# Layer 1's output gate, summed over partitions by block transposes and a selection matrix and spread through DRAM, in a two-layer diffusion trunk

## The chip, the core and the metric

The kernel runs on one core of one Trainium2 chip. The metric is device time in microseconds (us) for one execution. Before the change the median of three runs is 1133.07 us (1133.02 to 1134.05).

Engine names are those of the profile: PE is the matrix engine (PEld its weight loads), DVE the vector engine, ACT the scalar engine, POOL the general-purpose engine, SP the engine that issues nearly all DMA transfers. Each engine runs its own instructions in a fixed order. DMA transfers are issued by SP in that same manner: a transfer that has to wait for something holds back everything behind it on SP.

## The reference, cut to what matters

Two layers of the block below run on a latent stream of 256 tokens and a context of 256 tokens, width 2048, all in float32. The change concerns only the line that makes `gate` for the second layer (l = 1) and its use in the last line.

```python
for l in range(DEPTH):                      # DEPTH = 2
    shift, scale, gate = jnp.split(silu_c @ w_mod[l] + b_mod[l], 3, axis=-1)
    ...
    h = rmsnorm(x, g_pre[l]) * (1.0 + scale[:, None]) + shift[:, None]
    proj = h @ w_in[l]
    ...
    y = mixer_branches(proj, latent_attn, g_sgu[l], w_sgu[l], b_sgu[l], w_fourier[l], b_fourier[l])
    y = rmsnorm(y @ w_out[l], g_post[l])
    x_new = x + gate[:, None] * y
```

So `gate` of layer 1 is a vector of 2048 values: a product of a vector of 2048 with a 2048 x 2048 matrix, plus a bias. The kernel multiplies it by `g_post[1]` at once, and uses the product on every token row of the last projection's result.

## The kernel before

**The last stage.** `finish()` (from line 1134) is the last projection, `y @ w_out[1]`. The 2048 output columns are done in four chunks c of 512. In a chunk, the contraction runs over 16 tiles k of 128, and for each k two token tiles t of 128 rows are done; one product is three matmuls (high times high, high times low, low times high), since every float32 operand is split into two parts of a faster type. In chunk 3 the second token tile runs 8 steps of k behind the first (`BACK = 8`), so that the first one's result can be written out while the second is still being multiplied.

**The weight stream.** `W` loads weights in units of 512 KB; a unit of this stage holds two tiles k of one chunk, so a chunk takes eight units. A unit passes through three steps: SP issues the load into one of three `raw` buffers (line 433), ACT casts the high part out of it (`whi`, line 456), DVE subtracts to get the low part (`wlo`, line 458), after which the `raw` buffer is free. Four `whi` and four `wlo` buffers hold the split units until PE has used them. The last six units go to other places (`TAIL`, line 383), because chunk 3 keeps its units for a second pass: the pair hl0 to hl3, the pair hl4 to hl7, mraw, then macc with `ws bsb`, and two in yo buffers. So the tags `ws` and `bsb` are used in two ways: by the gate, and as the low part of the fourth of these units.

**The gate.** `mod_gate1` (line 280) makes the product with the matrix on DVE, in between other work: for each chunk c it accumulates 16 multiply-adds (lines 289 and 291) of 128 x 512 into a tile (`ctrh`, `ctrl`, `nstrh`, `nstrl` for c = 0 to 3). What is left is a sum over the 128 partitions. `gate1(c)` (line 298) does that, with the bias and `g_post`:

- SP loads two rows, bias and `g_post`, each spread to all 128 partitions, 256 KB each (line 302), into `ws` and `bsb`.
- ACT and DVE split the accumulated tile into two parts (lines 505 and 506).
- PE multiplies a matrix of ones by both parts (line 307), two matmuls of 512 columns. Every partition of the result then has the sum.
- DVE adds the bias row (line 308) and multiplies by the `g_post` row (line 309).

**Who uses it.** `evac(c, t)` (line 1166) multiplies the projection's result by `g1[c]` on DVE (line 1170) for c = 0 to 2, as soon as the 16 steps of one token tile are done; `close(t)` (line 1176) does it for c = 3 (line 1183) and writes the outputs.

**The order.** PE's order is written out by hand. Work that runs beside the matmuls is a generator handed to `later`; each step k moves the planner's clock on, and a generator goes on at the next step after its delay. `GATES` (line 336) says after which step each gate is begun: gate 0 after k = 2 of chunk 0, gate 1 after k = 14 of chunk 0, gate 2 after k = 14 of chunk 1, gate 3 after k = 12 of chunk 2. Between the two parts of `gate1` lie 6.5 planner units (`YG`), some six steps k. On the other engines and on SP the order is made by a list scheduler at build time, from its own estimate of when each instruction can run. So on SP a transfer may stand ahead of its place in the program text, but once the order is made, it is kept.

A second routine, `mod_end` (line 270), already sums other modulation vectors over partitions in another way: two DVE instructions of `mod_dve` (lines 259 and 260) transpose the accumulated tile in blocks of 32 x 32 and sum 32 elements each, and four small matmuls with the 128 x 32 selection matrix `selq` (line 273) add up the four blocks of partitions and put the result into columns, one value a partition. `Mod.cols` (line 189) uses the same four matmuls (line 193) with four columns.

Of the kernel before, what the change touches and what calls it, by code (L numbers as in the profile page):

```python
# [7 lines left out]
F32 = mybir.dt.float32  # L8
F32R = mybir.dt.float32r
BF16 = mybir.dt.bfloat16  # L10
AF = mybir.ActivationFunctionType
ALU = mybir.AluOpType

P = 128
# [52 lines left out]
def trunk_kernel(ctx: ExitStack, tc: tile.TileContext, xT, xhalf, cT, wss, wsl, wmod, win, wout0, wout1, const, vec, rows,  # L67
                 wmat, bs, sink, out):
    nc = tc.nc
    V, A, G, PE, DMA = nc.vector, nc.scalar, nc.gpsimd, nc.tensor, nc.sync  # L70

    pool = ctx.enter_context(tc.tile_pool(name="sb", bufs=1))
    psum = ctx.enter_context(tc.tile_pool(name="ps", bufs=1, space=bass.MemoryType.PSUM))
    W2K = 7
    cnt = [0]

    def sb(shape, dt, tag, bufs=1):
        cnt[0] += 1
        return pool.tile(shape, dt, tag=tag, bufs=bufs, name=f"{tag}_{cnt[0]}")

    def w2k(shape, dt=F32):
        return sb(shape, dt, "w2k", W2K)

# [4 lines left out]
    def ms_ps(name="ms"):  # L88
        cnt[0] += 1
        return psum.tile([P, 512], F32, tag="ms", bufs=2, name=f"ps_{name}_{cnt[0]}")  # L90
# [6 lines left out]
    ones = sb([P, P], F32, "ones")  # L97
# [29 lines left out]
    def cc(name):  # L127
        o, w = COFF[name]
        return cst[:, o - P:o - P + w]

    def vc(l, name):
        o, w = VOFF[name]
        return vecs[:, l, o:o + w]
# [8 lines left out]
    g1 = []  # L142
# [154 lines left out]

    def gate1(c):

        r = [sb([P, 512], F32, tag) for tag in ("ws", "bsb")]  # L300
        for i in range(2):
            DMA.dma_start(r[i], rows[None, i, c * 512:(c + 1) * 512].to_broadcast([P, 512]))
        parts = split_into(w2k([P, 512], F32R), w2k([P, 512], F32R), g1[c])
        yield YG
        ps = ms_ps("gate")
        for i, t in enumerate(parts):
            PE.matmul(ps, state["ones"], t, start=i == 0, stop=i == 1)
        V.tensor_tensor(out=g1[c], in0=r[0], in1=ps, op=ALU.add)
        V.tensor_tensor(out=g1[c], in0=g1[c], in1=r[1], op=ALU.mult)
        yield 0.0  # L310

    def mod_rest():
# [7 lines left out]
    state = {"ctx": [], "phase": "", "owed": 0.0}  # L320
# [183 lines left out]
    def split_into(hi, lo, src):  # L504
        A.copy(hi, src)  # L505
        V.tensor_tensor(out=lo, in0=src, in1=hi.bitcast(F32), op=ALU.subtract)  # L506
        return hi, lo
# [626 lines left out]
    def finish():  # L1134
# [68 lines left out]
        for c in range(4):  # L1203
            pss = [mm_ps("y") for _ in range(2)]
            back = BACK if c == 3 else 0
            w = []
            for k in range(KT + back):
                if k < KT:
                    if k % 2 == 0:
                        w.append(W.next())  # L1210
                    products(c, k, 0, pss[0])
                if k == KT - 1:
                    evac(c, 0, pss[0])
                    if c == 3:
                        close(0, pss[0])
                if k >= back:
                    products(c, k - back, 1, pss[1])
                later.tick(PASS * 1024)
                if k in GATES[c]:
                    later.add(gate1(GATES[c][k]))  # L1220
            evac(c, 1, pss[1])
# [93 lines left out]
    with tc.manual_schedule(engines={EN.PE}):  # L1315
# [12 lines left out]
        for k in range(KT):  # L1328
            q = w2k([P, T])
# [3 lines left out]
            c = slice(32 * (k % 4), 32 * (k % 4) + 32)  # L1333
# [3 lines left out]
        row = w2k([P, T])  # L1337
# [6 lines left out]
        ps = ms_ps("rs")  # L1344
# [99 lines left out]
```

## Time and profile before

| | us |
|---|---|
| median of three runs | 1133.07 |
| lowest and highest run | 1133.02, 1134.05 |
| the profiled execution's own time | 1132.31 |
| its span, first to last instruction | 1130.5 |
| PE busy | 1122.0 |
| DVE busy | 927.6 |
| ACT busy | 528.5 |
| chunks 0, 1, 2 of the last stage begin on PE at about | 1029.5, 1053.7, 1077.9 |
| chunk 3 begins, and PE's last product ends, at about | 1100.0, 1122.7 |

Times inside the trace count from the first instruction of the profiled execution. A row of a timeline has the start, the length, the engine, the line of the kernel, the operation, and output and input tiles; a bracket at its end tells how long the engine was idle before it and what ended that. In a matmul's row the length is that of one instruction from its start to its end in a pipeline; the distance from one start to the next is what it costs PE. The granted clock of PE reads 1.00 in all four chunks.

### The profile page before, as it was taken

Reading aid. Unit: us, or ns where it says so; the run is one execution under the profiler, and the core shown is the slowest. Engines: PE = TensorE matmul, PEld = TensorE weight load, DVE = VectorE, ACT = ScalarE, POOL = GpSimd, SP = SyncE. Lnnn points to the kernel's source line nnn. Section 1 sums busy time; section 2 is a strip of 40 time slices with the busy share of each in tenths; the row PEclk is TensorE's granted clock in tenths of the full one; section 3 lists DMA queues with packets and bytes.
Section 4 is the critical chain, followed back from the end, with each engine's and each line's share of the span. In section 5 each row is a group of like instructions: output and inputs, shape, how many; then the busy total and the mean of one; then the engine's idle time right before and its main releaser. Section 6 shows DMA issues by size and latency. Waiting matters only on the chain.

```text
span 1130.5 us, 16656 instructions
## 1 busy us (share of the span) xinstructions
PE 1122.0 (99%) x6117; PEld 921.5 (82%) x6117; DVE 927.6 (82%) x1649; ACT 528.5 (47%) x991; POOL 33.7 (3%) x41
## 2 busy tenths in 40 slices
PE   8999999999999999999999999999999999999998
PEld 3666788888888888888888888988888888888886
DVE  1578799989888788898999988397889789878883
ACT  5322433322235666642533334256665369857551
POOL 0000000000000000000000000030500000000000
PEclk9999999999999999999999999999999999999999
DMA  9999656566656344356556665276956686556972
GB/s 350 403 402 400 243 181 202 170 206 192 215 175 188 107 140 131 122 180 211 186 170 223 221 212 179 94 170 213 226 168 197 214 295 195 158 170 198 315 251 75
DMA packets 75250, 235.85 MB, mean 209 GB/s; under 512 B 8736, under 2 KB 13216, under 8 KB 75168
## 3 DMA queue, kind: packets, MB, share of 16 engines
q1 hardware_dynamic: 70992, 230.85, 61.4%
q0 software_dynamic: 4032, 3.67, 2.2%
q8 instruction: 48, 0.79, 0.3%
q14 instruction: 34, 0.28, 0.1%
q10 hardware_dynamic: 144, 0.26, 0.1%
HBM read 232.65 MB, written 2.10 MB: 208 GB/s over the span
## 4 chain that ended last, share of the span: by engine, by line
PE 96%; DVE 1%; ACT 1%; DMA 0%; issue 0%; SPq 0%; POOLq 0%; DVEq 0%; ACTq 0%
PE ps_t L488 15%; PE ps_t L490 15%; PE ps_t L489 15%; PE ps_t L604 10%; PE ps_t L605 5%; PE ps_v L1053 3%; PE ps_y L488 3%; PE ps_y L490 3%; PE ps_y L489 3%; PE ps_mod L181 2%; PE ps_av L488 2%; PE ps_av L489 2%; PE ps_av L490 2%; PE ps_tp L995 1%; PE ps_v L1054 1%; PE ps_au L488 1%
## 5 line engine op out<-in xcount | busy, mean ns | idle before, releaser
L456 ACT CAST whi<-raw 128x1024 fp32r<-128x1024 f32 (+1 forms) x209 | 216.4, 1037 | 320.6 <-PE ps_t L489 221.9
L488 PE MATMUL ps_t<-hh,whi 128*128 128x512 f32 (+1 forms) x752 | 290.6, 386 | 0.0
L490 PE MATMUL ps_t<-hh,wlo 128*128 128x512 f32 (+1 forms) x752 | 289.7, 385 | 0.0
L489 PE MATMUL ps_t<-hl,whi 128*128 128x512 f32 (+1 forms) x752 | 289.6, 385 | 0.0
L458 DVE TENSOR_TENSOR wlo<-raw,whi 128x1024 fp32r<-128x1024 f32 (+1 forms) x209 | 250.9, 1203 | 45.8 <-ACT whi L456 40.0
L253 DVE SCALAR_TENSOR_TENSOR macc<-mraw,cs,macc 128x512 f32<-128x512 f32 x360 | 250.0, 745 | 11.5 <-DMA mraw<-in_wmod_dram 11.2
L604 PE MATMUL ps_t<-hh,whi 128*128 128x512 f32 x512 | 184.9, 399 | 0.0
L490 PEld LDWEIGHTS ps_t<-hh,wlo 128*128 128x128 f32 x752 | 141.3, 188 | 28.5
L488 PEld LDWEIGHTS ps_t<-hh,whi 128*128 128x128 f32 x752 | 141.3, 188 | 26.9
L489 PEld LDWEIGHTS ps_t<-hl,whi 128*128 128x128 f32 x752 | 141.3, 188 | 26.4
L605 PE MATMUL ps_t<-hh,wlo 128*128 128x256 f32 x512 | 143.4, 280 | 0.0
L604 PEld LDWEIGHTS ps_t<-hh,whi 128*128 128x128 f32 x512 | 96.2, 188 | 21.5
L605 PEld LDWEIGHTS ps_t<-hh,wlo 128*128 128x128 f32 x512 | 96.6, 189 | 0.4
L570 ACT ACTIVATE hh<-w2k,sh 128x256 fp32r<-128x256 f32 x48 | 22.1, 503 | 72.7 <-DVE w2k L566 72.7
L488 PE MATMUL ps_y<-whi,hh 128*128 128x512 f32 x104 | 41.3, 397 | 0.0
L490 PE MATMUL ps_y<-whi,hh 128*128 128x512 f32 x104 | 40.6, 390 | 0.0
L489 PE MATMUL ps_y<-wlo,hh 128*128 128x512 f32 x104 | 40.5, 389 | 0.0
L488 PE MATMUL ps_av<-whi,hh 128*128 128x512 f32 x94 | 39.0, 415 | 0.6 <-ACT hh L570 0.6
L489 PE MATMUL ps_av<-wlo,hh 128*128 128x512 f32 x94 | 37.1, 395 | 0.0
L505 ACT CAST w2k<-ps_tp 128x512 fp32r<-128x512 f32 x40 | 23.4, 586 | 20.3 <-PE ps_scc L489 8.6
L518 POOL TENSOR_TENSOR rs_b<-rs_a,mhalf 128x2 f32<-128x2 f32 (+1 forms) x6 | 6.6, 1096 | 776.8 <-DVE mx L1245 584.8
L506 DVE TENSOR_TENSOR w2k<-ps_tp,w2k 128x512 fp32r<-128x512 f32 x40 | 27.4, 684 | 1.3 <-ACT w2k L505 0.5
(458 smaller groups left out, 1777.0 us busy)
## 6 DMA issues: line engine op xcount, KB each, us to landing
raw<-in_win_dram SPq DMA_DIRECT2D x160, 512.0 KB, 4.1
mraw<-in_wmod_dram SPq DMA_DIRECT2D x128, 512.0 KB, 4.2
raw<-in_wout_dram SPq DMA_DIRECT2D x60, 512.0 KB, 4.4
mraw<-in_wsl_dram SPq DMA_DIRECT2D x14, 512.0 KB, 7.2
yo<-in_xT_dram SPq DMA_DIRECT2D x16, 256.0 KB, 5.3
yo<-in_wsl_dram SPq DMA_DIRECT2D x16, 256.0 KB, 7.2
macc<-in_wsl_dram SPq DMA_DIRECT2D x7, 512.0 KB, 7.7
vv<-in_wsl_dram SPq DMA_DIRECT2D x7, 512.0 KB, 8.4
```

Source lines behind the costliest of these rows:

```text
L181: PE.matmul(self.ps[32 * kk:32 * kk + 32, 0:self.N], cpad[:, kg * 4 + kk], self.w[kg * 4 + kk], start=kg == 0, stop=kg == 3, tile_position ...
L253: V.scalar_tensor_tensor(out=acc[:, s], in0=w[:, kk % 2], scalar=c, in1=acc[:, s], op0=ALU.mult, op1=ALU.add)
L456: A.copy(ph, rc)
L458: self.last = V.tensor_tensor(out=pl, in0=rc, in1=ph.bitcast(F32), op=ALU.subtract)
L488: PE.matmul(ps, st[0], mv[0], start=start, stop=False)
L489: PE.matmul(ps, st[0], mv[1], start=False, stop=False)
L490: PE.matmul(ps, st[1], mv[0], start=False, stop=stop)
L505: A.copy(hi, src)
L506: V.tensor_tensor(out=lo, in0=src, in1=hi.bitcast(F32), op=ALU.subtract)
L604: PE.matmul(ps, w[0], h, start=k == 0, stop=False)
L605: PE.matmul(ps[:, 0:S], w[1], h[:, 0:S], start=False, stop=k == KT - 1)
L1053: PE.matmul(vps[t], hi, wk, start=k == 0, stop=False)
```

## The change

`gate1` is rewritten; nothing else is but for a DRAM pool. The two row loads and the split are gone. The accumulated tile is transposed in blocks and reduced to 16 columns on DVE, as `mod_dve` does. After the same delay, four small matmuls with `selq` bring the sums into four columns, one value a partition. Bias and `g_post` come from the column form of the vectors that lies in SBUF since the start (`vc`), so DVE adds and multiplies 128 x 4 elements in place of 128 x 512. The four columns are then written to a DRAM tile of 512 values, element by element (the value of partition p, column j goes to place 128 j + p), and a second transfer reads that row and spreads it to all partitions. The second transfer waits for the first one, and both are issued by SP. The tile `g1[c]` is a new one with the same tag as the accumulator.

```diff
+    dram = ctx.enter_context(tc.tile_pool(name="dram", bufs=1, space=bass.MemoryType.DRAM))
...
     def gate1(c):
 
-        r = [sb([P, 512], F32, tag) for tag in ("ws", "bsb")]
-        for i in range(2):
-            DMA.dma_start(r[i], rows[None, i, c * 512:(c + 1) * 512].to_broadcast([P, 512]))
-        parts = split_into(w2k([P, 512], F32R), w2k([P, 512], F32R), g1[c])
+        tag = ("ctrh", "ctrl", "nstrh", "nstrl")[c]
+        red, t = sb([P, 16], F32, "red", 2), w2k([P, 512])
+        V.transpose(t, g1[c])
+        V.tensor_reduce(out=red, in_=t.rearrange("p (b j) -> p b j", j=32), axis=mybir.AxisListType.X, op=ALU.add)
         yield YG
         ps = ms_ps("gate")
-        for i, t in enumerate(parts):
-            PE.matmul(ps, state["ones"], t, start=i == 0, stop=i == 1)
-        V.tensor_tensor(out=g1[c], in0=r[0], in1=ps, op=ALU.add)
-        V.tensor_tensor(out=g1[c], in0=g1[c], in1=r[1], op=ALU.mult)
+        for q in range(4):
+            PE.matmul(ps[32 * q:32 * q + 32, 0:4], cc("selq"), red.rearrange("p (j q) -> p j q", q=4)[:, :, q],
+                      start=True, stop=True, tile_position=(0, 32 * q))
+        col = sb([P, 4], F32, "mx", 2)
+        V.tensor_tensor(out=col, in0=ps[:, 0:4], in1=vc(1, "bmod")[:, 32 + 4 * c:36 + 4 * c], op=ALU.add)
+        V.tensor_tensor(out=col, in0=col, in1=vc(1, "gpost")[:, 4 * c:4 * c + 4], op=ALU.mult)
+        row = dram.tile([4, P], F32, tag=f"gate{c}", name=f"gate{c}")
+        with nc.allow_non_contiguous_dma(reason="512 values"):
+            DMA.dma_start(row.rearrange("j p -> p j"), col)
+        g1[c] = sb([P, 4, P], F32, tag)
+        DMA.dma_start(g1[c], row[None].to_broadcast([P, 4, P]))
+        g1[c] = g1[c].rearrange("p j f -> p (j f)")
         yield 0.0
```

## The prediction

> **What bounds the kernel now.** I read the page first: the span, the engines' shares, and the chain of work that ended last.
>
> ```profile
> span 1130.5 us, 16656 instructions
> PE 1122.0 (99%) x6117; PEld 921.5 (82%) x6117; DVE 927.6 (82%) x1649; ACT 528.5 (47%) x991; POOL 33.7 (3%) x41
> PE 96%; DVE 1%; ACT 1%; DMA 0%; issue 0%; SPq 0%; POOLq 0%; DVEq 0%; ACTq 0%
> ```
>
> PE is the chain. Whatever the change does to another engine counts only where PE then waits. So next the waits of PE over the last 230 us, and after it the stretches of chunks 1, 2 and 3 (start:end, length, then busy us and count for PE, PEld, DVE, ACT, POOL, then clock, DMA share, GB/s).
>
> ```profile
> PE ps_x L1194 <- ACT w2k L1186: 0.5, 1, 0.5
> PE ps_sc L490 <- DVE w2k L506: 0.4, 1, 0.4
> 1053.70:1077.90 24.20, 24.20 (x114) 20.03 (x113) 21.71 (x28) 14.35 (x22) 0.00 (x0) 1.00 0.94 332
> 1077.90:1100.05 22.15, 22.15 (x99) 18.32 (x98) 19.45 (x25) 11.29 (x17) 0.00 (x0) 1.00 0.82 264
> 1100.05:1122.65 22.60, 22.60 (x99) 18.41 (x98) 8.96 (x19) 2.99 (x8) 0.55 (x1) 1.00 0.12 46
> ```
>
> PE waits 0.9 us in all, and none of it is for the gate. Its busy time equals the length of each stretch. But the supply behind it is nearly full: in chunk 1 DVE is busy 21.71 of 24.20 us (90%) and the DMA engines 94%; in chunk 2 it is 88% and 82%. So there is nothing to win beside PE's own work, and there is something to lose if the supply is held up.
>
> **PE's own part.** Timeline rows around gate 0, and around four selection matmuls of 4 columns in the first stage (each shows as two rows, so eight):
>
> ```profile
> 1044.34 0.39 PE L490 MATMUL ps_y<-whi,hh 128*128 128x512 f32 x1
> 1044.57 0.62 PE L307 MATMUL ps_gate<-w2k,join 128*128 128x512 f32 x2
> 1045.03 0.40 PE L488 MATMUL ps_y<-whi,hh 128*128 128x512 f32 x1
> 1045.27 0.39 PE L489 MATMUL ps_y<-wlo,hh 128*128 128x512 f32 x1
> ```
>
> ```profile
> 130.65 0.40 PE L490 MATMUL ps_av<-whi,hl 128*128 128x512 f32 x1
> 130.97 0.24 PE L193 MATMUL ps_modc<-w2k,cst 128*32 128x4 f32 x8
> 131.15 0.50 PE L488 MATMUL ps_au<-hh,whi 128*128 128x512 f32 x1
> 131.49 0.40 PE L489 MATMUL ps_au<-hl,whi 128*128 128x512 f32 x1
> ```
>
> ```profile
> 1103.24 0.39 PE L488 MATMUL ps_y<-hl,hh 128*128 128x512 f32 x1
> 1104.60 0.39 PE L488 MATMUL ps_y<-hl,hh 128*128 128x512 f32 x1
> ```
>
> The last two rows lie six matmuls apart, 1.36 us, so a step costs PE 0.227 us. From L490 to L489 at gate 0 is 0.93 us where two steps would take 0.454: the old pair costs 0.476 us. In the first stage the same distance is 0.84 us: the new four cost 0.386, slow start of the next matmul included. The gain is 0.09 us a gate, 0.36 us for four. Bounds: nothing if changing forms costs as much as the old pair; at most 0.476 - 0.24 = 0.24 a gate (the eight rows alone), 0.9 us in all. I take 0.36, from the group of the same shape.
>
> **ACT and DVE.** The new front is one transpose and one reduction of 128 x 512 (L259, L260), the new back two operations on 4 columns; the nearest row is L150 with 8. Removed are a cast on ACT and three operations of DVE (L506, L308, L309).
>
> ```profile
> L259 DVE STREAM_TRANSPOSE mraw<-macc x24: 657/702/714, 177.6 to 693.3; 128x512 f32<-128x512 f32 x24
> L260 DVE TENSOR_REDUCE red<-mraw x24: 643/678/687, 178.4 to 694.0; 128x16 f32<-128x512 f32 x24
> L150 DVE TENSOR_TENSOR sh<-ps_modc,vecs x4: 156/156/167, 703.2 to 703.5; 128x8 f32<-128x8 f32 x4
> L505 ACT CAST w2k<-nstrl x1: 617/617/617, 1089.8 to 1089.8; 128x512 fp32r<-128x512 f32 x1
> 1089.35 0.68 DVE L308 TENSOR_TENSOR nstrh<-ws,ps_gate 128x512 f32<-128x512 f32 x1
> 1091.08 0.68 DVE L309 TENSOR_TENSOR nstrh<-nstrh,bsb 128x512 f32<-128x512 f32 x1
> 1091.68 0.68 DVE L506 TENSOR_TENSOR w2k<-nstrl,w2k 128x512 fp32r<-128x512 f32 x1
> ```
>
> Per gate DVE goes from 3 x 0.68 = 2.04 us to 0.70 + 0.68 + 2 x 0.16 = 1.70, and ACT loses 0.62. Four gates: 1.4 us less on DVE, 2.5 us less on ACT. PE waits for neither, so I cost both at nothing; they would count only if the supply ran late. That the low part for `ws` need no longer wait for gate 3 to read it is worth nothing either, for the same reason.
>
> **The way through DRAM.** This is the price of the change. What was ready with L309 now needs a store of 512 single values, its landing, a spread of 256 KB, and that one's landing. The rows with which to bound it:
>
> ```profile
> ct<-in_cT_dram SPq DMA_DIRECT2D x1, 16.0 KB, 1.7
> DMA to landing us min/median/max: 3.4/4.5/5.7
> DMA to landing us min/median/max: 3.6/4.8/6.0
> q0 software_dynamic: 4032, 3.67, 2.2%
> ```
>
> The first is the shortest way of any load; the second is the old row loads (L302, as large as the new spread); the third the weight loads from 1070 us on. No row shows a store of single values. Queue q0 moved packets of 910 bytes, and 2.2% of 16 engines' 1130.5 us over 4032 packets is 0.099 us each. With 512 elements on 16 engines that is 32 x 0.099 = 3.2 us an engine. So the store's landing D lies between 1.7 us (elements cost nothing, empty queue) and 6.0 + 3.2 = 9.2 us (behind the slowest load, every element at a packet's price). I take 5: 1.7 + 3.2, a little for what stands ahead. The spread takes 4.5 (3.4 to 5.7). With two issues of 0.33 us the value is on all partitions 10.2 us after the columns, between 5.8 and 15.6.
>
> [...]
>
> Is that late? Gate 0 is the tight one:
>
> ```profile
> 1045.95 0.68 DVE L308 TENSOR_TENSOR ctrh<-ws,ps_gate 128x512 f32<-128x512 f32 x1
> 1055.03 0.68 DVE L1170 TENSOR_TENSOR yo<-ps_y,ctrh 128x512 f32<-128x512 f32 x1
> 1102.34 0.68 DVE L1170 TENSOR_TENSOR yo<-ps_y,nstrh 128x512 f32<-128x512 f32 x1
> ACT whi L456 <- PE ps_y L490: 12.3, 10, 2.2
> ```
>
> Columns at 1045.95 + 0.3 = 1046.3, the spread value at 1056.5 (1052.1 to 1061.9), first wanted at 1055.03: DVE stands for 1.5 us (0 to 6.9). Behind it wait the next gate's front and the low parts of weight units. In this stretch ACT's casts wait ten times for PE to free a buffer, so units are split as early as four buffers let them be: a unit just cast is wanted three units later, and a unit is 12 matmuls, 2.72 us. That is 8.2 us less a cast of 1.05 and a subtraction of 1.22, with some queueing about 5 us of cover. 1.5 us is hidden. Gate 2 has its columns at 1089.65 and is wanted at 1102.34, 12.7 us against 10.2. Gates 1 and 3 have some 13 us.
>
> **SP.** Every transfer behind the spread waits on SP until the store has landed, weight loads among them. The point where that matters is the start of chunk 3, where only one token tile is multiplied and PE takes a unit in 1.36 us:
>
> ```profile
> 1091.19 0.33 SPq L433 DMA_DIRECT2D raw<-in_wout_dram  x1
> 1094.13 2.06 SPq L433 DMA_DIRECT2D raw<-in_wout_dram  x2
> 1096.70 1.23 DVE L458 TENSOR_TENSOR wlo<-raw,whi 128x1024 fp32r<-128x1024 f32 x1 [0.86 <-ACT whi L456]
> 1098.82 1.29 DVE L458 TENSOR_TENSOR hl<-raw,hl 128x512 fp32r<-128x512 f32 x2 [0.89 <-ACT hl L456]
> 1101.12 1.29 DVE L458 TENSOR_TENSOR hl<-raw,hl 128x512 fp32r<-128x512 f32 x2 [1.01 <-ACT hl L456]
> 1101.64 0.39 PE L489 MATMUL ps_y<-wlo,hh 128*128 128x512 f32 x1
> ```
>
> The three loads become the three DVE units. The unit in hl0 to hl3 is split at 1100.11 and wanted at 1103.24: 3.1 us to spare. The next: 1102.41 against 1104.60, 2.2 us. The one before: 1097.93 against 1101.64, 3.7 us. With gate 2's store issued at 1089.65, SP is held until 1089.98 + D, the spread's own issue included. If the load of 1091.19 stands ahead of the spread in SP's order, as its buffer comes free before a store could have landed, then D = 5 delays the load of 1094.13 by 0.9 us and the last, at 1095.86, not at all. Covered.
>
> **The sum**: 1132.31 - 0.36 = 1131.95 us for the profiled execution. That execution stands 0.76 us under the median, so in the median 1133.07 - 0.36 = 1132.7.
>
> **Rivals.**
>
> First, and on the other side: SP held at gate 2 starves chunk 3. From 1089.98 + D - 1094.13 > 3.1 on, so for D above 7.3, PE waits for the hl unit; at D = 9.2 the wait is 1.9 us. If the scheduler puts the spread ahead of the load of 1091.19, the delay is D - 1.2 against 3.7 to spare: from D = 4.9, and 4.3 us at 9.2. For it speaks that loads there are already what ACT waits for, and that held matrix loads at gates 0 and 1 would cost DVE time which at 90% it cannot make up; against it that at 5 us D reaches neither point by much. The middle is 3.1 us: 1132.7 + 3.1 = 1135.8, and with both ends bad 1138. [...] No row here shows a transfer that waits for another's store in mid-kernel.
>
> Second: DVE held at gate 0. At the far end it stands 6.9 us against 5 of cover, and PE waits 2: 1134.7. It needs a store near 9 us too, in chunk 0, where nothing else presses.
>
> Third: the new matmuls cost PE only their busy time, 0.9 us gained, 1132.2; or as much as the old pair, 1133.1, so that the change does nothing on PE.
>
> **How the numbers follow.** Forecast 0.62, first rival 0.26, second 0.06, third 0.06. A measurement here can tell about 0.2%, 2.3 us, from no change. Forecast, second and third lie within it but for a rest of 0.03 on the faster side; all of the first is taken as beyond. So faster 0.03, same 0.71, slower 0.26. The range runs from 1131.6 (the 0.9 us and a run's scatter) to 1138; the likeliest case alone holds 1131.8 to 1133.8.
>
> **What would show it.** Right: ps_gate with sixteen 128 x 4 matmuls' worth of rows at 0.39 us a group; no wait of PE on `wlo` or hl at the start of chunk 3; a wait of SP on the gate's DRAM tile of about 5 us, four times; DVE standing 1 to 2 us before its first L1170. Wrong: PE rows with idle time at 1100 to 1106 released by DVE or ACT, chunk 3 beginning or ending later against chunk 2, a store landing after more than 7 us, or the spread standing ahead of weight loads whose buffers were free.

## The result, and the profile after

| | us |
|---|---|
| median before, after (four runs each) | 1133.37, 1150.87 |
| ratio, 95% interval | 1.0156, 1.0141 to 1.0171 |
| span before, after | 1130.5, 1148.3 |

The change makes the kernel 1.6% slower, some 17.5 us. The forecast of 1132.7 and the range up to 1138 are both missed. The page of the changed kernel, the lines that answer to those of before:

```profile
span 1148.3 us, 16702 instructions
PE 1128.7 (98%) x6141; PEld 924.6 (81%) x6141; DVE 925.7 (81%) x1653; ACT 525.6 (46%) x987; POOL 33.7 (3%) x41
DMA packets 76786, 234.81 MB, mean 204 GB/s; under 512 B 10784, under 2 KB 15264, under 8 KB 76704
PE 89%; DMA 5%; DVE 4%; ACT 2%; issue 1%; SPq 0%; POOLq 0%; DVEq 0%; ACTq 0%
```

The chain that ended last is no longer PE nearly alone: DMA holds 5% of it. Packets under 512 bytes went from 8736 to 10784, which is 2048 more, four stores of 512 values. The waits of PE in the last 250 us (who waited, for whom, total, times, longest):

```profile
PE ps_y L498 <- DVE wlo L467: 7.8, 2, 5.4
PE ps_gate L308 <- ACT mgl L1157: 1.9, 1, 1.9
PE ps_y L497 <- ACT whi L465: 1.4, 1, 1.4
```

That is 11.1 us of new waits; the last stage of the kernel before had only the 0.5 us at its end. The other 6.7 us are PE's busy time, 1128.7 against 1122.0. It is not more work: around three of its waits here PE runs for a while at a granted clock of 0.50. Counted by matmul products, 96 to a chunk, chunk 1 takes 27.3 us in place of 23.7 and chunk 2 36.6 in place of 22.2; chunks 0 and 3 take as long as before. Two-microsecond stretches around the longest wait (length, busy and count of PE, clock, DMA share, GB/s), and rows of PE's timeline behind it:

```profile
1108.00:1110.00 2.00, 0.00 (x0) 1.00 0.90 49
1110.00:1112.00 2.00, 0.00 (x0) 0.67 0.69 53
1112.00:1114.00 2.00, 0.70 (x2) 0.50 0.65 214
1114.00:1116.00 2.00, 2.00 (x6) 0.50 0.87 146
1116.00:1118.00 2.00, 2.00 (x7) 0.62 0.92 270
1118.00:1120.00 2.00, 2.00 (x11) 1.00 0.44 178
```

```profile
1113.30 0.80 PE L498 MATMUL ps_y<-wlo,hh 128*128 128x512 f32 x1 [5.43 <-DVE wlo L467]
1113.89 0.63 PE L499 MATMUL ps_y<-whi,hh 128*128 128x512 f32 x1
1114.32 0.63 PE L497 MATMUL ps_y<-whi,hh 128*128 128x512 f32 x1
```

Here the granted clock falls to half while PE stands, and a matmul costs 0.43 us until some 4 us after work has begun again, against 0.227 before. The clock is at half in three stretches of the last stage: 1066.3 to 1069.7 us, 1086.8 to 1093.6 and 1110.7 to 1117.5. The first begins 1.1 us after a wait of only 1.92 us has ended. PE works for about 3.4, 5.2 and 4.2 us in them; half of that, 6.4 us, is an estimate of what the slow clock cost.

Why was the low part late? The transfers issued between 1046 and 1056.4 us, the stretch of gate 0's store (destination, source, count, size, us to landing), and SP's waits for the store in the last stage:

```profile
raw<-in_wout_dram SPq DMA_DIRECT2D x1, 512.0 KB, 12.6
mraw<-in_wmod_dram SPq DMA_DIRECT2D x1, 512.0 KB, 13.5
gate<-mx SPq DMA_DIRECT2D x1, 2.0 KB, 10.1
```

```profile
SPq L317 <- DMA gate<-mx: 35.2, 4, 10.2
```

The store of 2 KB takes 10.1 us. SP stands for it 35.2 us over four gates. And the two loads that SP issued behind the store, but ahead of the spread, one of weights and one of the gate's matrix, took 12.6 and 13.5 us; over the whole kernel such loads have medians of 4.3 and 4.2. DVE, in its fixed order, stands for each gate matrix load that is late, and the low parts of the weight units stand behind that (the bracket is DVE's wait):

```profile
1061.41 0.75 DVE L292 SCALAR_TENSOR_TENSOR nstrh<-mraw,cs,nstrh 128x512 f32<-128x512 f32 x1 [8.06 <-DMA mraw<-in_wmod_dram]
1085.69 1.54 DVE L292 SCALAR_TENSOR_TENSOR nstrl<-mraw,cs,nstrl 128x512 f32<-128x512 f32 x2 [6.49 <-DMA mraw<-in_wmod_dram]
1111.36 0.75 DVE L292 SCALAR_TENSOR_TENSOR nstrl<-mraw,cs,nstrl 128x512 f32<-128x512 f32 x1 [6.57 <-DMA mraw<-in_wmod_dram]
```

The third of these leads to PE's wait of 5.43 us. In the chain of work that ended last (start, us, what), the pieces at gates 0 and 2 are:

```profile
1046.30 10.13 DMA gate<-mx
1056.87 6.65 DMA raw<-in_wout_dram
1098.92 12.35 DMA mraw<-in_wmod_dram
```

At gate 0 the chain goes through the store, SP's wait for it and a load issued behind the spread. At gate 2 it goes through a matrix load that was issued 1.4 us ahead of the store (1100.33) and took 12.35 us all the same. So there are two suspects: SP standing (theory B, the prediction's first rival) and the store holding back the other transfers (theory A). In gate 3, with no weight loads left, it is as slow:

```profile
1123.58 0.38 SPq L315 DMA_DIRECT2D gate<-mx  x1
1132.46 0.33 SPq L317 DMA_DIRECT2D nstrl<-gate  x1
```

8.9 us from issue to the spread's issue, which waits for the landing alone.

### The profile page after: what moved, and what is told of

It is laid out like the page before. It is cut to its first block, busy times and chain, and to the rows that moved or that the text cites. A ratio compares the mean times of both kernels' runs of the same rounds, so it can differ in the third digit from the quotient of the medians.

```text
span 1148.3 us, 16702 instructions
## 1 busy us (share of the span) xinstructions
PE 1128.7 (98%) x6141; PEld 924.6 (81%) x6141; DVE 925.7 (81%) x1653; ACT 525.6 (46%) x987; POOL 33.7 (3%) x41
## 2 busy tenths in 40 slices
DMA packets 76786, 234.81 MB, mean 204 GB/s; under 512 B 10784, under 2 KB 15264, under 8 KB 76704
## 4 chain that ended last, share of the span: by engine, by line
PE 89%; DMA 5%; DVE 4%; ACT 2%; issue 1%; SPq 0%; POOLq 0%; DVEq 0%; ACTq 0%
PE ps_t L497 15%; PE ps_t L499 15%; PE ps_t L498 15%; PE ps_t L613 10%; PE ps_t L614 5%; PE ps_v L1062 3%; PE ps_mod L182 2%; PE ps_av L497 2%; PE ps_av L498 2%; PE ps_av L499 2%; DMA gate<-mx 2%; DMA raw<-in_wout_dram 1%; PE ps_tp L1004 1%; DVE wlo L467 1%; PE ps_v L1063 1%; PE ps_au L497 1%
## 5 line engine op out<-in xcount | busy, mean ns | idle before, releaser
L499 PE MATMUL ps_t<-hh,wlo 128*128 128x512 f32 (+1 forms) x752 | 289.7, 385 | 0.0
L498 PE MATMUL ps_t<-hl,whi 128*128 128x512 f32 (+1 forms) x752 | 289.7, 385 | 0.0
L499 PEld LDWEIGHTS ps_t<-hh,wlo 128*128 128x128 f32 x752 | 141.3, 188 | 28.7
L498 PEld LDWEIGHTS ps_t<-hl,whi 128*128 128x128 f32 x752 | 141.3, 188 | 26.5
L498 PE MATMUL ps_y<-wlo,hh 128*128 128x512 f32 x104 | 43.4, 418 | 7.8 <-DVE wlo L467 7.8
L497 PE MATMUL ps_y<-whi,hh 128*128 128x512 f32 x104 | 44.1, 424 | 1.4 <-ACT whi L465 1.4
L499 PE MATMUL ps_y<-whi,hh 128*128 128x512 f32 x104 | 42.9, 412 | 0.0
L498 PE MATMUL ps_av<-wlo,hh 128*128 128x512 f32 x94 | 37.1, 395 | 0.0
L498 PEld LDWEIGHTS ps_y<-wlo,hh 128*128 128x128 f32 x104 | 21.2, 204 | 12.8 <-DVE wlo L467 8.7
```

The source lines that it names most:

```text
L497: PE.matmul(ps, st[0], mv[0], start=start, stop=False)
L498: PE.matmul(ps, st[0], mv[1], start=False, stop=False)
L499: PE.matmul(ps, st[1], mv[0], start=False, stop=stop)
```

## The experiments

**The store as four rows.** Undoes the form of the store alone, at the price of one more matmul a gate.

```diff
+        yield 2.0
+        PE.matmul(ps[0:4, P:2 * P], col, ident, start=True, stop=True)
+        flat = w2k([P, P])
+        A.copy(flat[0:4], ps[0:4, P:2 * P])
...
-            DMA.dma_start(row.rearrange("j p -> p j"), col)
+            DMA.dma_start(row, flat[0:4])
```

> The columns are turned into four rows of 128 by one more small matmul before the store, so that the store is 4 runs of 512 bytes in place of 512 single values; everything else as in the changed kernel (SP issues both transfers, the spread waits for the store). Theory A (the single values fill every DMA engine's queue, and weight loads behind them stand): the store lands in 2 to 2.5 us in place of 8.9 to 11.8, PE's waits at chunks 2 and 3 go, and the time is 1133 to 1135 us. Theory B (SP stands while the spread waits for the store, and that alone starves PE): the same, as the wait shrinks with the landing. Theory C (the way through DRAM costs whatever the form: a written row that is read back and spread): the store still lands after 7 us or more and the time stays above 1145.

Measured: 1135.64 us, ratio 1.0018 (1.0008 to 1.0028). All but 2.4 us of the loss is gone. Gate 3's store and spread, and the one new wait of PE that is left in the stage:

```profile
1108.07 0.27 SPq L319 DMA_DIRECT2D gate<-w2k  x1
1109.24 0.33 SPq L321 DMA_DIRECT2D nstrl<-gate  x1
```

```profile
PE ps_gate L314 <- DVE mx L312: 1.4, 1, 1.4
```

This store lands within 1.2 us. The wait is for the added matmul, placed too early, and with the added work PE is busy 1124.0 us against 1122.0. So theory C, the way through DRAM as such, is out; A and B are not told apart.

**SP freed, the store's queue changed, and both.** Three kernels: the spread issued by POOL (first pair of lines), the store issued by ACT (second pair), both.

```diff
-        DMA.dma_start(g1[c], row[None].to_broadcast([P, 4, P]))
+        G.dma_start(g1[c], row[None].to_broadcast([P, 4, P]))
...
-            DMA.dma_start(row.rearrange("j p -> p j"), col)
+            A.dma_start(row.rearrange("j p -> p j"), col)
```

> The spread is issued by POOL, which does nothing else here, so that SP does not stand for the store; the store of 512 single values stays on SP. Theory A (queue filled by the store): loads issued just after the store still land after 10 us or more, PE still waits, and the time is 1143 to 1151 us. Theory B (SP standing alone): the waits of PE go and the time is 1133 to 1136. Both at work by halves: 1139 to 1145.

> The store of 512 single values is issued by ACT, so that it lies in another queue than the weight loads; the spread stays on SP and SP stands for it as before. Theory B (SP standing alone): as the changed kernel, 1147 to 1152 us. Theory A in the form that loads stand behind the store in their own queue: loads issued before the spread land in about 5 us, and the time falls to 1138 to 1146, the rest being SP's wait. Theory A in the form that the single values take the engines' time whatever the queue: loads still land after 8 us or more, and the time stays at 1147 to 1152 as under B, but with slow loads in the trace.

> The store of 512 single values is issued by ACT and the spread by POOL: SP never stands, and the weight loads have their queue to themselves. If queue order and SP's wait are all there is (A as queue order, with B): 1133 to 1135 us. If the single values take the engines' time whatever the queue: loads in the store's stretch still land late, and the time is 1138 to 1148, not below the run with the spread on POOL by more than 3 us.

Measured:

| | us | ratio, 95% interval |
|---|---|---|
| spread on POOL | 1155.62 | 1.0193, 1.0178 to 1.0208 |
| store on ACT | 1155.71 | 1.0201, 1.0186 to 1.0217 |
| both | 1155.56 | 1.0189, 1.0166 to 1.0212 |

All three lie above every range that was expected, and none is better than the changed kernel. With both moved, SP never stands for the store and the weight loads share no queue with the store. Transfers of that kernel issued between 1079 and 1091 us, the stretch of gate 1's store:

```profile
raw<-in_wout_dram SPq DMA_DIRECT2D x3, 512.0 KB, 11.2
mraw<-in_wmod_dram SPq DMA_DIRECT2D x2, 512.0 KB, 10.6
gate<-mx ACTq DMA_DIRECT2D x1, 2.0 KB, 11.8
```

The loads still take 11 us. Taking SP's wait away wins nothing, and another queue wins nothing: in the last 5 us of this store, which was issued at 1079.67 us, little else moves. From 1086 to 1091 us all engines together move 45 GB/s; the kernel before moves 301 GB/s from 1076 to 1082.8. So theory B alone is not the cause, and of theory A the form that holds whatever the queue stands. Whether it is the 16 engines that are held or the DRAM behind them is not shown. Why these three are some 4 us slower still than the changed kernel was not settled; the scheduler's orders on DVE and ACT differ a little from it.

**Half the values.**

```diff
-        row = dram.tile([4, P], F32, tag=f"gate{c}", name=f"gate{c}")
+        row = dram.tile([2, P], F32, tag=f"gate{c}", name=f"gate{c}")
...
-            DMA.dma_start(row.rearrange("j p -> p j"), col)
+            DMA.dma_start(row.rearrange("j p -> p j"), col[:, 0:2])
...
-        DMA.dma_start(g1[c], row[None].to_broadcast([P, 4, P]))
+        for i in range(2):
+            DMA.dma_start(g1[c][:, 2 * i:2 * i + 2], row[None].to_broadcast([P, 2, P]))
```

> Only two of the four columns are stored, 256 single values, and both halves of a chunk are filled with them, so half of the gate's factors are left out. Theory A with a price for each value: gate 3's store lands in 1.7 + 16 x 0.22 = 5.3 us; PE's buffers cover most of it, and the time is 1133 to 1141 us. If the store's price were fixed (a way through DRAM, a written row read back): it lands in 8 us or more and the time stays above 1147.

Measured: 1153.98 us, ratio 1.0180 (1.0165 to 1.0195). Half the values cost as much. Gate 3:

```profile
1128.63 0.38 SPq L315 DMA_DIRECT2D gate<-mx  x1
1136.97 0.80 SPq L318 DMA_DIRECT2D nstrl<-gate  x2
```

8.3 us in place of 5.3. So theory A was wrong about the price: it is not so much a value. This run came out as a fixed price for a way through DRAM would have it; the run with four rows and the next one speak against that.

**The columns as they lie.** 128 runs of 16 bytes, the same 2 KB.

```diff
-        row = dram.tile([4, P], F32, tag=f"gate{c}", name=f"gate{c}")
+        row = dram.tile([P, 4], F32, tag=f"gate{c}", name=f"gate{c}")
...
-            DMA.dma_start(row.rearrange("j p -> p j"), col)
+            DMA.dma_start(row, col)
...
-        DMA.dma_start(g1[c], row[None].to_broadcast([P, 4, P]))
+        DMA.dma_start(g1[c].rearrange("p j f -> p (j f)"), row.rearrange("p j -> (p j)")[None].to_broadcast([P, 512]))
```

> The four columns are stored as they lie, 128 runs of 16 bytes, 8 to an engine in place of 32 single values, and the row is read back in that order, so that the gate's 512 factors of a chunk come in another order than the reference's. Theory A, a price for each run whatever its length (0.22 us, from 8.9 us for 32 in the empty queue of gate 3 less 1.7): the store lands in 3 to 4 us and the time is 1132 to 1137 us. If it is the single values' 4 bytes of DRAM written piece by piece (2 KB in either form) that cost, and not the runs: it lands after 7 us or more and the time is above 1145.

Measured: 1133.81 us, ratio 1.0001 (0.9992 to 1.0010). The whole loss is gone, and every engine and SP have the same instructions in the same order as in the changed kernel. This is the cleanest pair of the study: only the shape of four stores of 2 KB differs. The spread is written as one row of 512 in place of four of 128, but moves as many packets: the whole kernel has 1536 fewer, which is 4 x (512 - 128). The stores land in 3.7 us at the median, and SP's wait for them falls to 6.9 us in all:

```profile
gate<-mx SPq DMA_DIRECT2D x4, 2.0 KB, 3.7
```

```profile
SPq L317 <- DMA gate<-mx: 6.9, 4, 2.2
```

**Without DRAM.** The way through DRAM undone alone.

```diff
+        yield 2.0
+        for j in range(4):
+            PE.matmul(ps[:, j * P:(j + 1) * P], col[:, j:j + 1].to_broadcast([P, P]), ident, start=True, stop=True)
...
+        A.copy(g1[c], ps.rearrange("p (j f) -> p j f", f=P))
```

> The way through DRAM is undone alone: four matmuls of 128 x 128 with the identity spread each column to all partitions, and ACT copies the result out. The transposes, the selection matmuls and the scaling as columns stay. Theory A (and B): nothing is left that holds the weight loads; PE pays some 0.6 us a gate more than in the changed kernel, and with a wait of 1 to 2 us for the columns the time is 1134 to 1138 us. If the block transposes and selection matmuls had a share in the loss, PE's waits on the low parts stay and the time is 1140 or more.

Measured: 1137.37 us, ratio 1.0033 (1.0021 to 1.0044). PE waits for no low part in the last stage, so transposes, reductions and selection matmuls have no share in the loss. From the first matmul product of the stage to the last are 96.3 us against 92.9 in the kernel before: 3.4 of the 3.9 us that are left go with PE's added work. The profiled execution, the slowest of seven, also reaches the last stage 4.5 us later than the kernel before, ahead of any of the gates' sums; why is not known.

**The store measured by itself.** The kernel before, with small transfers behind its last output, each waiting for the one before.

```diff
+            pa = dram.tile([4, P], F32, tag="pa", name="pa")
+            pb = dram.tile([P, 4], F32, tag="pb", name="pb")
+            pc = dram.tile([P, 1], F32, tag="pc", name="pc")
...
+                DMA.dma_start(pa.rearrange("j p -> p j"), src)
+                DMA.dma_start(q[0], pa.rearrange("j p -> p j"))
+                DMA.dma_start(pb, q[0])
+                DMA.dma_start(q[1], pb)
+                DMA.dma_start(pc, q[1][:, 0:1])
+                DMA.dma_start(q[2][:, 0:1], pc)
```

> The kernel before, with a chain of six small transfers behind its last output, each waiting for the one before, with nothing else on the DMA engines; only their landing times are of interest, and the time is longer by their sum. In order: 512 single values to DRAM, 512 single values from DRAM, 128 runs of 16 bytes to DRAM and from DRAM, 128 single values to DRAM and from DRAM. Price for each run, writes alone: 8.9, about 2, 3.5, 2, 3.5, 2 us. Price for each run in both directions: 8.9, 8.9, 3.5, 3.5, 3.5, 3.5. A fixed price of a small write to DRAM: all three writes near 8.9.

```profile
pa<-yo SPq DMA_DIRECT2D x1, 2.0 KB, 9.4
skb<-pa SPq DMA_DIRECT2D x1, 2.0 KB, 4.1
pb<-skb SPq DMA_DIRECT2D x1, 2.0 KB, 2.0
nskb<-pb SPq DMA_DIRECT2D x1, 2.0 KB, 2.0
pc<-nskb SPq DMA_DIRECT2D x1, 0.5 KB, 7.6
tot<-pc SPq DMA_DIRECT2D x1, 0.5 KB, 3.4
```

Each landing here and in the next run was measured in one execution. 512 single values take 9.4 us to DRAM, 128 take 7.6, and 128 runs of 16 bytes take 2.0. None of the three expectations fits: the price goes neither with the number of runs nor with a small store as such. What is left is the single value of 4 bytes, or its lying beside others (theory D).

**Distance, and a load behind the store.** The same, 128 pieces each time, read back after each store. `step(w, d)` stores one piece of w values from each partition, d values apart in DRAM.

```diff
+                step(4, 4, "pr16")
+                step(2, 2, "pr8")
+                step(1, 1, "pr4")
+                step(1, 4, "sp16")
+                step(1, 16, "sp64")
+                step(1, 128, "sp512")
+                st = step(1, 1, "beh4")
+                with tc.issue_after(st.ins):
+                    DMA.dma_start(sb([P, 1024], F32, "macc"), win[0, 0, 0])
+                st = step(1, 128, "beh512")
+                with tc.issue_after(st.ins):
+                    DMA.dma_start(sb([P, 1024], F32, "mraw", 2), win[0, 0, 1])
```

> The kernel before, with a chain of small transfers behind its last output, each store followed by a load that reads it back and waits for it: 128 pieces each time, of 16, 8 and 4 bytes side by side, then of 4 bytes at distances of 16, 64 and 512 bytes; then 4 bytes side by side and 4 bytes at 512, each with a load of 512 KB issued right behind it. Only the landing times matter. If what costs is pieces written side by side into the same stretch of DRAM: 2, 2 to 5, 7.6 us, then falling to 2 to 3 us at 512 bytes. If it is the piece of 4 bytes itself: 7.6 us at every distance. If the store holds the engines for other transfers: the load behind the side-by-side store lands after 8 us or more, the one behind a fast store after 3 to 4; if the store is only slow to be confirmed, both land in 3 to 4 us.

SP's timeline: L1184 is a store, L1185 the load that waits for it, so the distance from one to the next is the landing.

```profile
1128.54 0.45 SPq L1184 DMA_DIRECT2D pr<-yo  x1
1131.50 0.33 SPq L1185 DMA_DIRECT2D w2k<-pr  x1
1133.83 0.32 SPq L1184 DMA_DIRECT2D pr<-w2k  x1
1136.59 0.32 SPq L1185 DMA_DIRECT2D w2k<-pr  x1
1139.27 0.32 SPq L1184 DMA_DIRECT2D pr<-w2k  x1
1146.21 0.32 SPq L1185 DMA_DIRECT2D w2k<-pr  x1
1150.02 0.32 SPq L1184 DMA_DIRECT2D sp<-w2k  x1
1152.07 0.32 SPq L1185 DMA_DIRECT2D w2k<-sp  x1
1154.06 0.32 SPq L1184 DMA_DIRECT2D sp<-w2k  x1
1155.46 0.32 SPq L1185 DMA_DIRECT2D w2k<-sp  x1
1156.97 0.32 SPq L1184 DMA_DIRECT2D sp<-w2k  x1
1158.37 0.32 SPq L1185 DMA_DIRECT2D w2k<-sp  x1
```

Side by side, pieces of 16, 8 and 4 bytes take 3.0, 2.8 and 6.9 us. Pieces of 4 bytes at a distance of 16, 64 and 512 bytes take 2.1, 1.4 and 1.4. So a piece of 4 bytes is not slow by itself; pieces of 4 bytes that adjoin one another in DRAM are. The landings go as well with how many pieces crowd into one stretch of DRAM: with 1 piece in 64 bytes 1.4 us, with 4 pieces 2.0 to 3.0, with 8 pieces 2.8, with 16 pieces 6.9 to 7.6. Which of the two counts, and why, was not told apart. The 512 KB loads issued right behind a store:

```profile
macc<-in_win_dram SPq DMA_DIRECT2D x1, 512.0 KB, 11.7
mraw<-in_win_dram SPq DMA_DIRECT2D x1, 512.0 KB, 3.8
```

11.7 us behind the adjoining pieces, 3.8 behind the spaced ones, with nothing but the small read-back beside them and SP waiting for nothing between. The first load lands 3.6 us after the store has landed, about what the second takes in all. The slow store holds the load back.

**A mended version.** Stores as in the run with runs of 16 bytes; DVE reads the factors in the order in which they now lie.

```diff
-        g1[c] = g1[c].rearrange("p j f -> p (j f)")
+        g1[c] = g1[c].rearrange("p j f -> p (j f)").rearrange("p (f j) -> p j f", j=4)
...
-                V.tensor_tensor(out=gy[c, t], in0=ps, in1=g1[c], op=ALU.mult)
+                V.tensor_tensor(out=four(gy[c, t]), in0=four(ps), in1=g1[c], op=ALU.mult)
```

> The columns are stored as they lie, 128 runs of 16 bytes, and the row is read back in that order; the multiplications of lines 1170 and 1183 read the factors through a view with a step of four elements, so that every factor meets its own column. The order of all transfers on SP is that of the changed kernel. Theory D (the price is that of pieces of 4 bytes written side by side to DRAM, which hold the engines about 8 us whatever their number): the store lands in 2 to 5 us, PE waits nowhere in the last stage, and the time is that of the kernel before less at most 0.4 us: a ratio of 0.998 to 1.001. If the view costs DVE much more than 0.68 us a multiplication, the tail grows by that and the time is 1 to 2 us above. Theory B (SP's wait for the store): SP still waits some 2 us four times, so some of the loss would stay.

Measured: 1133.24 us against 1133.38 for the kernel before, ratio 0.9997 (0.9988 to 1.0006): no difference that can be told. PE waits nowhere in the last stage but for the 0.5 us at its end that the kernel before has too. Reading with a step of four elements costs DVE 1.05 us in place of 0.68:

```profile
L1182 DVE TENSOR_TENSOR yo<-ps_y,ctrh 128x512 f32<-128x512 f32 x2 | 2.1, 1049 | 0.0
```

## Why the prediction was wrong

**PE's own part was right.** Around gate 3 in the changed kernel, L499 starts at 1120.37 and L498 behind the selection matmuls at 1121.21: 0.84 us, as in the row of the first stage. The sum of the profile's forecast, no more than a few tenths gained, fits the mended version: there the last stage's products take 92.67 us from first to last against 92.91, 0.24 of the forecast 0.36. A gain of that size is within the interval of the times.

**ACT and DVE at nothing: right.** The run without DRAM keeps all of that work, and there PE waits for nothing in the last stage that the kernel before did not.

**The step that failed is the landing D of the store**: "So the store's landing D lies between 1.7 us (...) and 6.0 + 3.2 = 9.2 us (...). I take 5". Measured were 10.1, 10.3 and 11.8 us at gates 0, 1 and 2, above the end that was to hold even behind the slowest load, and 8.9 in the empty queue of gate 3, where the same working gives 1.7 + 3.2 = 4.9. The working took a packet's time from a queue with packets of 910 bytes and multiplied by the number of pieces. The runs show that the number hardly counts (7.6 us for 128, 8.3 for 256, 8.9 to 9.4 for 512), and that what counts is how closely pieces of 4 bytes lie. No row of the kernel before had such a store, so its upper bound was not one.

**What D does was misread too.** The prediction let it act on two things, the arrival of the gate's factors and SP's place in line. It priced the second for what is issued behind the spread, and called a load ahead of the spread safe. The trace shows loads ahead of it landing after 12.6 and 13.5 us, a load ahead of the store itself after 12.35, and the kernel with both transfers moved away from SP is no faster. Loads already issued, or issued in another queue, were not thought of as being held. With the 11.8 us of gate 2, the first rival's own working gives 1089.98 + 11.8 - 1094.13 - 3.1 = 4.6 us, where the change cost 17.5: the size of D alone does not account for the loss. The first rival had the right side, but the wrong hold and the wrong place. It expected the loss in chunk 3; chunk 3 lost nothing, while chunk 1 lost 3.6 us and chunk 2 14.3. Its remark that held matrix loads would cost DVE time is what came true, at gates 0, 1 and 2.

**Left out altogether: PE's clock around a wait.** The price of a wait was taken as its length. Here 11.1 us of waits came with some 6.4 us lost in matmuls at a granted clock of 0.50 (the estimate above).

**The second rival, DVE at gate 0.** DVE did stand, but for matrix loads held by the store (8.06 us, until L292 at 1061.41), not for the factors. The factors landed 5.8 us behind the spread's issue at 1056.45, at about 1062.2, past the prediction's far end of 1061.9.

**Still open**: whether SP standing for 9 us, with the engines free, would have cost anything. It was not tried; in the mended version SP stands up to 3 us at a time and PE loses nothing. Also open: whether adjoining or crowding makes the store slow, and whether the engines or the DRAM are held.

## What to carry to other kernels

Before a small store is put beside a full load stream, look at how its pieces lie in DRAM, not only at its bytes: here the same 2 KB cost nothing as 128 runs of 16 bytes and 17 us as 512 adjoining single values. Keep the order in which data lie in SBUF and let a later reader take the permutation: 0.37 us a multiplication on DVE was free here. And a bound taken from rows of another shape of transfer is a guess; where the kernel's margin hangs on it, measure that transfer alone at the end of the kernel first.

## What the runs showed of the hardware that was not expected

- Adjoining 4-byte pieces to DRAM: 128 of them land after 6.9 to 7.6 us (8.4 with a 512 KB load issued behind them), 512 after 8.9 to 9.4 (10.1 to 11.8 at gates 0 to 2, beside loads); at a distance of 16 bytes 2.1 us, at 64 bytes 1.4.
- Such a store holds other transfers, also those in another queue: a 512 KB load behind it in SP's queue lands after 11.7 us, and after 3.8 behind a store of spaced pieces; with the store in ACT's queue, loads in SP's take 11 us. A load issued 1.4 us ahead of such a store took 12.35 us.
- Reading adjoining 4-byte pieces from DRAM into 128 partitions was slower than runs of 16 bytes as well, 3.4 to 4.1 us against 2.0 to 2.3; spaced 4-byte pieces took 1.5 at the median of three.
- PE's granted clock fell to half in three stretches of 3.4, 6.8 and 6.8 us, two of them begun while PE stood, one 1.1 us after a wait of 1.92 us.
